# Value projection of eight heads as seven block products, with the raw values parked in DRAM

## The chip, the cores and the metric

One core of one Trainium2 chip runs the whole kernel. The metric is the device time of one launch in microseconds; the clock of TensorE and the busy time of each engine are read from one profiled execution.

## What is computed

Two decoder layers over 512 positions of width 2048. In each layer one projection of x gives queries, keys, values and gates of 12 self-attention heads (six with a forget bias, six sparse with a top-128 selection by an indexer), indexer queries and keys, and queries and gates of four heads into a memory of 256 tokens. The change touches the values alone:

```python
(fq, fk, fv, fg, f_logit, dq, dk, dv, dg, iq, ik, iw, mq, mg) = jnp.split(h, offsets, axis=-1)   # h = x @ w_in
...
y_fox = fox_attention(heads(fq, H_FOX), heads(fk, H_FOX), heads(fv, H_FOX), cum_logf)
...
y = jnp.concatenate([y_fox, y_dsa, y_mem], axis=-1)
y = jnp.einsum('bsn,nd->bsd', y, w_out)
return layer_norm(ALPHA * x + y, ln_gain, ln_bias)
```

All values are float32. Products run as three float32r products of split operands (high times high, high times low, low times high).

## The kernel before, in words

**Chunks.** All weights lie in DRAM as a row of chunks of 128 x 2048 numbers (1 MB). Of each layer the order is: `mv` x4 and `mk` x4 (values and keys of the memory), four pairs `mq`, `mg`, then `small`, `iq` x8 (indexer), and per self-attention head a gate, a query and a key chunk; ahead of heads 0, 4 and 8 stand four `val` chunks that give the values of four heads (512 columns). The output projection (`out`) ends the layer. It already runs as seven products of blocks for each pair of column blocks (Strassen-Winograd, table `PRODUCTS`), with its sums of weight blocks T1 to T4 made beforehand by DMAs from DRAM to DRAM that add on the way (`weight_sums`, on GpSimd's queue). `pool_waits` paces them: a tiny copy on VectorE, then a tiny product on GpSimd, then the DMA.

**The stream.** The main loop goes over the chunks; half a chunk (`h` 0 or 1) has number n. At its start `load_w(i + 2)` issues the load of a later chunk on SyncE's queue, `split_w(n + 3)` splits a later half (ScalarE writes the high part `whi`, VectorE the low part `wlo`), then come the matmuls. There are three raw buffers and four for split halves, so TensorE's splits run at most three halves ahead. Each engine, SyncE's queue too, takes its instructions in the order in which the program issues them.

**Ticks.** Side work (attention, indexer, sums, operands, `next_x`) is a set of generators; `tick()` lets each make a step after either half of a chunk. With `half` it passes over those begun with `whole=True`.

**Slots.** All other tiles of 128 x 512 come from one pool of 69 slots. An instruction whose output finds no free slot waits, on its engine, until one is given back.

**Values.** A `val` chunk has 48 matmuls with 512 columns (two halves, four blocks of rows, two blocks of the sum, three products each). Behind the fourth one the four banks are split at once into `vh`, `vl`, which the heads read.

**Layer change.** `next_x` normalises the residual, transposes it back (16 blocks k, two per tick, during `mv` and `mk` of layer 1), and makes `xf` and its split `xh`, `xl`: 32 slots that hold x of the layer.

Of the kernel before, what the change touches and what calls it, by code (L numbers as in the profile page):

```python
# [11 lines left out]
F32 = mybir.dt.float32  # L12
F32R = mybir.dt.float32r
# [4 lines left out]
P = 128  # L18
# [48 lines left out]

OUT_ORDER = (("P1", 0), ("P1", 1), ("P7", 0), ("P7", 1), ("Q6", 0), ("Q6", 1), ("Q4", 0), ("Q4", 1),
             ("Q5", 0), ("Q5", 1), ("P2", 0), ("Q3", 0), ("P2", 1), ("Q3", 1))


def layer_chunks(l):

    out = []
    for j in range(H_MEM):
        out += [("mq", l, j, MQ + j * HD), ("mg", l, j, MG + j * HD)]
    out.append(("small", l, 0, None))
    for j in range(8):
        out.append(("iq", l, j, IQ + j * P))
    for n in range(H_FOX + H_DSA):  # L80
        if n % 4 == 0:
            out += [("val", l, n // 4, g) for g in range(4)]
        if n < H_FOX:
            h, kinds = n, (("fg", FG), ("fq", FQ), ("fk", FK))
        else:
            h, kinds = n - H_FOX, (("dg", DG), ("dq", DQ), ("dk", DK))
        out += [(kind, l, h, base + h * HD) for kind, base in kinds]
    for dc in range(4):
        for g in range(4):
            out.append(("out", l, dc, g))  # L90
    return out
# [12 lines left out]
def stream():  # L104

    wall = all_chunks()
    where = {c: i for i, c in enumerate(wall)}
    out = []
    for i, c in enumerate(wall):
        kind, l = c[:2]  # L110
        if kind != "out":
            out.append((*c, ("wall", i)))
        elif c == ("out", l, 0, 0):
            for name, pair in OUT_ORDER:
                right = PRODUCTS[name][2]
                for g in range(2):
                    if isinstance(right, str):
                        src = ("sum", (l, right, pair, g))
                    else:
                        src = ("wall", where["out", l, 2 * pair + right[1], 2 * right[0] + g])  # L120
                    out.append((kind, l, (name, pair), g, src))
    return out


# [15 lines left out]
def kernel(  # L140
# [156 lines left out]
    def weight_sums(l):  # L297

        every = [(pair, g) for pair in range(2) for g in range(2)]
        for name, first, second in (("T1", (0, 0), (0, 1)), ("T3", (0, 1), (1, 1)),  # L300
                                    ("T2", "T1", (1, 1)), ("T4", "T2", (1, 0))):
            for step in (first, second):
                for pair, g in every:
                    key = (l, name, pair, g)
                    if isinstance(step, str):
                        src = sums[l, step, pair, g]
                    else:
                        src = wall[where["out", l, 2 * pair + step[1], 2 * step[0] + g]]
                    pool_waits()
                    if step is second:  # L310
# [4 lines left out]
                    yield 2  # L315

    crow_d = [dram.tile([H_FOX, SEQ], F32, name=f"crow{l}") for l in range(DEPTH)]
    x1_d = dram.tile([SEQ, DM], F32, name="x1")


    active = []

    def begin(gen, wait=0, last=False, whole=False):


        active.append([wait, gen, last, whole])

    def tick(half=False):
        for a in sorted(active, key=lambda a: a[2]):
            if half and a[3]:  # L330
                continue
            if a[0] > 0:
                a[0] -= 1
# [304 lines left out]
            yield 1  # L638


    z, stats = {}, {}

    def load_res(l, st, dc):
# [25 lines left out]
    def next_x():  # L669

        ms = [norm_stats(st) for st in range(4)]
        for c in range(4):
            for st in range(4):
                normalise(st, c, *ms[st])
            yield 1
        for k in range(KT):
            c, o = divmod(k, 4)
            tp = bank("xt")
            for st in range(4):
                nc.tensor.transpose(tp[:, st * P:(st + 1) * P], z[st, c][:, o * P:(o + 1) * P], ident)  # L680
            xf, hi, lo = slot("xf"), slot("xh", F32R), slot("xl", F32R)
            nc.scalar.activation(xf, tp, AF.Identity, bias=gcol[:, 1, k:k + 1],
                                 scale=gcol[:, 0, k:k + 1])
            nc.scalar.activation(hi, xf, AF.Copy)
            eng = nc.gpsimd if k % 2 else nc.vector
            eng.tensor_tensor(lo, xf, hi.bitcast(F32), op=ALU.subtract)
            xT[k] = (hi, lo)
            if k % 2:
                yield 1
        yield 6  # L690
        load_rows(0)
        yield 2
# [75 lines left out]
    def weight_cols(n, kk):  # L768
        return tuple(a[:, kk * P:(kk + 1) * P] for a in parts[n])

    for i, (kind, l, j, col, _) in enumerate(chunks):
        late = last_half(i)
        if kind == "out":
            step = OUT_ORDER.index(j)
            name, pair = j
            chain, aname, _, targets = PRODUCTS[name]
            opens = name in ("P1", "P2", "Q6")
            if col == 0:
                if opens:
                    chains[chain, pair] = [bank("z"), bank("z")]  # L780
                zs = chains[chain, pair]

                for st, dc in RES_LOADS.get(step, ()):
                    load_res(l, st, dc)
                if step == 2:
                    begin(late_operands())
        elif kind in ("val", "mv"):
            if col == 0:
                out_ps = {st: bank("v") for st in range(4 if kind == "val" else 2)}
        else:  # L790
            ps = bank("c")
        for h in range(2):
# [35 lines left out]
            elif kind == "out":  # L828
                for st in range(2):
                    for e in range(2):  # L830
                        r = slice(e * 256 + st * P, e * 256 + (st + 1) * P)
                        product(zs[st], tuple(a[:, r] for a in left[aname, 2 * col + h]),
                                tuple(a[:, e * 512:(e + 1) * 512] for a in parts[n]),
                                opens and col == h == e == 0,
                                col == h == e == 1, not opens)
            elif kind == "val":
                for st in range(4):
                    for nn in range(2):
# [24 lines left out]
                            k == 0, k == KT - 1)  # L863
            del parts[n]
            if h == 0:
                tick(kind == "out")
        if kind == "mk":
            t = slot("kmem", F32R)
            split(ps[:, :256], t[:, 0:256], t[:, 256:512])
# [16 lines left out]
        elif kind in ("mg", "fg", "dg"):  # L886
            gate((kind[0], j), ps)
        elif kind == "val" and col == 3:
            vs[j] = []
            for st in range(4):  # L890
                hi, lo = slot("vh", F32R), slot("vl", F32R)
                split(out_ps[st], hi, lo)
                vs[j].append((hi, lo))
        elif kind == "small":
            sm = slot("sm")
            nc.scalar.activation(sm, ps, AF.Copy)
# [128 lines left out]
```

## Time and profile before

| | us |
|---|---|
| median of 3 runs (1987.11 to 1987.69) | 1987.65 |
| the profiled execution, its own time | 1987.82 |
| its span, first to last instruction | 1986.0 |
| TensorE busy in the span | 1970.3 |
| VectorE, ScalarE, GpSimd busy | 1267.4, 732.2, 234.7 |

The profiled execution's own time is 1.8 us over its span (launch and end) and 0.2 us over the median. Busy time of TensorE counts matmuls whose ends are modelled; how densely they stand is read from their starts.

### The profile page before, as it was taken

The numbers are of one execution on the slowest core, as the hardware profiler recorded it, in microseconds if no ns is written. First come the engines' busy times: TensorE is split into PE (matmuls) and PEld (weight loads), VectorE is DVE, ScalarE is ACT, GpSimd is POOL, SyncE is SP. The second block draws the span as 40 slices with busy tenths as digits, with TensorE's granted clock in tenths as the row PEclk, the third lists the DMA queues.
The fourth block names the chain that finished last, engine by engine and source line by source line (L and its number), as shares of the span: only waits on it lengthen the run. The fifth ranks groups of instructions, "written<-read, shape, count | busy, mean of one in ns | idle before, by whom it ended". The sixth has DMA issues, their size and how long they took to land.

```text
span 1986.0 us, 24234 instructions
## 1 busy us (share of the span) xinstructions
PE 1970.3 (99%) x9506; PEld 1677.0 (84%) x9506; DVE 1267.4 (64%) x2069; ACT 732.2 (37%) x1156; POOL 234.7 (12%) x383
## 2 busy tenths in 40 slices
PE   9999999999999999999999999999999999999997
PEld 8889988888888888888898899888888888888886
DVE  6446755678446355688875567456784553567888
ACT  6333344323222222454472333342323232224453
POOL 0000101120110000100038201011201100001101
PEclk9999999999999999999999999999999999999999
DMA  9322355555745322466445324555657362224765
GB/s 371 117 85 78 114 191 133 203 160 191 189 169 151 109 85 85 149 219 241 176 161 200 106 87 156 161 159 181 170 175 199 145 174 102 85 85 164 274 216 151
DMA packets 49966, 316.18 MB, mean 159 GB/s; under 512 B 6576, under 2 KB 6576, under 8 KB 19388
## 3 DMA queue, kind: packets, MB, share of 16 engines
q1 hardware_dynamic: 37596, 226.53, 31.2%
q0 software_dynamic: 12256, 88.11, 17.3%
q8 instruction: 74, 1.21, 0.2%
q14 instruction: 40, 0.33, 0.1%
HBM read 306.20 MB, written 77.62 MB: 193 GB/s over the span
## 4 chain that ended last, share of the span: by engine, by line
PE 97%; DVE 1%; issue 1%; DMA 0%; SPq 0%; ACT 0%; POOL 0%; POOLq 0%; DVEq 0%
PE c L187 20%; PE c L189 19%; PE c L188 19%; PE v L189 5%; PE v L187 5%; PE v L188 5%; PE z L188 5%; PE z L189 5%; PE z L187 5%; PE pt L576 1%; PE po L189 1%; PE po L188 1%; PE po L187 1%; PE ix L503 1%; PE ix L502 1%; PE s L188 1%
## 5 line engine op out<-in xcount | busy, mean ns | idle before, releaser
L187 PE MATMUL c<-xh,whi 128*128 128x512 f32 (+1 forms) x1696 | 650.0, 383 | 0.0
L189 PE MATMUL c<-xh,wlo 128*128 128x512 f32 (+1 forms) x1696 | 647.0, 381 | 0.0
L188 PE MATMUL c<-xl,whi 128*128 128x512 f32 (+1 forms) x1696 | 646.4, 381 | 0.0
L181 DVE TENSOR_TENSOR wlo<-raw,whi 128x1024 fp32r<-128x1024 f32 (+1 forms) x401 | 498.6, 1249 | 199.6 <-ACT whi L180 198.3
L180 ACT ACTIVATE whi<-raw 128x1024 fp32r<-128x1024 f32 (+1 forms) x401 | 419.6, 1052 | 305.1 <-PE v L189 81.8
L189 PEld LDWEIGHTS c<-xh,wlo 128*128 128x128 f32 x1696 | 318.4, 188 | 57.4 <-DVE wlo L181 0.3
L188 PEld LDWEIGHTS c<-xl,whi 128*128 128x128 f32 x1696 | 318.6, 188 | 54.7
L187 PEld LDWEIGHTS c<-xh,whi 128*128 128x128 f32 x1696 | 318.6, 188 | 54.4
L188 PE MATMUL z<-wlo,yh 128*128 128x512 f32 (+1 forms) x434 | 167.9, 387 | 1.2 <-DVE wlo L181 1.2
L187 PE MATMUL z<-whi,yh 128*128 128x512 f32 (+1 forms) x434 | 167.8, 387 | 0.0
L189 PE MATMUL z<-whi,yl 128*128 128x512 f32 (+1 forms) x434 | 167.6, 386 | 0.0
L187 PE MATMUL v<-whi,xh 128*128 128x512 f32 x384 | 150.2, 391 | 0.0
L189 PE MATMUL v<-whi,xl 128*128 128x512 f32 x384 | 149.7, 390 | 0.0
L188 PE MATMUL v<-wlo,xh 128*128 128x512 f32 x384 | 149.5, 389 | 0.0
L188 PEld LDWEIGHTS z<-wlo,yh 128*128 128x128 f32 x434 | 81.5, 188 | 18.3 <-DVE wlo L181 2.0
L189 PEld LDWEIGHTS z<-whi,yl 128*128 128x128 f32 x434 | 81.5, 188 | 16.4
L187 PEld LDWEIGHTS z<-whi,yh 128*128 128x128 f32 x434 | 81.5, 188 | 16.2
L295 POOL TENSOR_TENSOR seen<-mark,mhalf 128x1 f32<-128x1 f32 x64 | 13.6, 212 | 675.0 <-DVE mark L294 562.9
L189 PEld LDWEIGHTS v<-whi,xl 128*128 128x128 f32 x384 | 72.1, 188 | 15.2
L513 DVE SCALAR_TENSOR_TENSOR acc<-rel,iw,acc 128x256 f32<-128x256 f32 (+2 forms) x90 | 51.9, 615 | 51.6 <-ACT rel L507 51.6
L188 PEld LDWEIGHTS v<-wlo,xh 128*128 128x128 f32 x384 | 72.1, 188 | 14.8
L187 PEld LDWEIGHTS v<-whi,xh 128*128 128x128 f32 x384 | 72.1, 188 | 14.6
(175 smaller groups left out, 2259.2 us busy)
## 6 DMA issues: line engine op xcount, KB each, us to landing
raw<-in_wall_dram SPq DMA_DIRECT2D x167, 1024.0 KB, 5.2
sum<-in_wall_dram POOLq DMA_DIRECT2D x32, 1024.0 KB, 8.6
raw<-sum SPq DMA_DIRECT2D x32, 1024.0 KB, 4.8
memraw<-in_memt_dram SPq DMA_DIRECT2D x16, 256.0 KB, 5.3
xraw<-in_xt_dram SPq DMA_DIRECT2D x16, 256.0 KB, 9.0
z<-in_x_dram POOLq DMA_DIRECT2D x16, 256.0 KB, 5.7
x<-z POOLq DMA_DIRECT2D x16, 256.0 KB, 3.4
z<-x POOLq DMA_DIRECT2D x16, 256.0 KB, 6.4
```

What stands on the lines that cost most here:

```text
L180: nc.scalar.activation(hi, src, AF.Copy)
L181: nc.vector.tensor_tensor(lo, src, hi.bitcast(F32), op=ALU.subtract)
L187: nc.tensor.matmul(ps, ah, bh, start=start, stop=False, skip_group_check=more)
L188: nc.tensor.matmul(ps, ah, bl, start=False, stop=False, skip_group_check=more)
L189: nc.tensor.matmul(ps, al, bh, start=False, stop=stop, skip_group_check=more)
L295: nc.gpsimd.tensor_tensor(seen, mark, mhalf, op=ALU.mult)
L502: nc.tensor.matmul(o, st[:, qb * P:(qb + 1) * P], kh2[:, :w], start=True, stop=False)
L503: nc.tensor.matmul(o, st[:, qb * P:(qb + 1) * P], kl2[:, :w], start=False, stop=True)
L513: nc.vector.scalar_tensor_tensor(a, rel, wq, a, op0=ALU.mult, op1=ALU.add)
L576: nc.tensor.transpose(tp[tb][:, toff + (qb - kt) * P:toff + (qb - kt + 1) * P], pr[b][:, off + kt * P:off + (kt + 1) * P], ident)
```

## The change

The values of heads 0 to 7 (`val` chunks j = 0 and 1) are made right behind the memory heads' chunks, ahead of `small`, as one 512 x 2048 by 2048 x 1024 product in seven block products of two chunks each (kind `vs`, 24 matmuls a chunk, order P1, P2, Q6, P7, Q5, Q4, Q3). Weight sums T1 to T4 for them are made by the same kind of DMA (16 more of 1 MB in each layer), begun at chunk 8 in layer 0 (a step at every tick) and at the first chunk of layer 1 (a step at every second tick). The sums of x blocks (S1 to S4) are made by `val_operands` from x read again from DRAM: from the input in layer 0, in layer 1 from `xt_d`, to which `next_x` now writes each `xf` on SyncE's queue. The results are combined (`val_out`), written raw to DRAM (`v_d`), loaded again one chunk ahead of their heads (`load_v`) and split then (`split_v`). The third group of values is still made by `val` chunks, now ahead of head 6, kept raw, and split at head 8. The indexer's scores begin two `iq` chunks earlier, the sums for `out` begin at `small`, and `mem_head` is passed over at half ticks.

```diff
+VAL_ORDER = ("P1", "P2", "Q6", "P7", "Q5", "Q4", "Q3")
 def layer_chunks(l):
         out += [("mq", l, j, MQ + j * HD), ("mg", l, j, MG + j * HD)]
+    out += [("val", l, j, g) for j in range(2) for g in range(4)]
     out.append(("small", l, 0, None))
     for n in range(H_FOX + H_DSA):
-        if n % 4 == 0:
-            out += [("val", l, n // 4, g) for g in range(4)]
+        if n == H_FOX:
+            out += [("val", l, 2, g) for g in range(4)]
...
+    def load_vx(l, i, *blocks):
+        src = (xt_in if l == 0 else xt_d).rearrange("p (k t c) -> p k t c", k=KT, t=2)
+        for t, kh in blocks:
+            vx[t, kh, i] = slot("vx")
+            nc.sync.dma_start(vx[t, kh, i].rearrange("p (k c) -> p k c", k=2),
+                              src[:, 8 * kh + 2 * i:8 * kh + 2 * i + 2, t, :])
+    def val_operand(name, i, x):
+        vleft[name, i] = slot("vxh", F32R), slot("vxl", F32R)
+        split(x, *vleft[name, i])
+    def val_operands(l):
+        first = ((0, 0), (1, 0), (1, 1))
+        load_vx(l, 0, *first)
+        yield 1
+        for i in range(4):
+            if i < 3:
+                load_vx(l, i + 1, *first)
+            a11, a21, a22 = (vx.pop((*b, i)) for b in first)
+            nc.vector.tensor_tensor(a21, a11, a21, op=ALU.subtract)
+            nc.vector.tensor_tensor(a22, a21, a22, op=ALU.add)
+            vx["S3", i], vx["S2", i] = a21, a22
+            yield 1
+            val_operand("S2", i, a22)
+            yield 1
+        for i in range(4):
+            load_vx(l, i, (0, 0))
+            val_operand("S3", i, vx.pop(("S3", i)))
+            yield 1
...
+    def val_out(name, ps):
+        if name in ("P1", "P7", "Q6"):
+            for st in range(2):
+                vraw[name, st] = slot("vraw")
+                nc.scalar.activation(vraw[name, st], ps[st], AF.Copy)
+        for st in range(2):
+            if name == "P2":
+                vraw[0, st] = slot("vraw")
+                nc.vector.tensor_tensor(vraw[0, st], vraw["P1", st], ps[st], op=ALU.add)
+            elif name in ("Q4", "Q5", "Q3"):
+                first, key = {"Q4": ("Q6", (0, 2 + st)), "Q5": ("P7", (1, 2 + st)),
+                              "Q3": ("P1", (1, st))}[name]
+                t = vraw[key] = vraw.pop((first, st))
+                nc.vector.tensor_tensor(t, ps[st], t, op=ALU.subtract)
+        for key in [k for k in vraw if k[0] in (0, 1)]:
+            nc.sync.dma_start(v_d[key], vraw.pop(key))
+    def load_v(j):
+        for st in range(4):
+            vraw[j, st] = slot("vraw")
+            nc.sync.dma_start(vraw[j, st], v_d[j, st])
...
     def next_x():
             nc.scalar.activation(xf, tp, AF.Identity, bias=gcol[:, 1, k:k + 1],
                                  scale=gcol[:, 0, k:k + 1])
+            nc.sync.dma_start(xt_d[:, k * SEQ:(k + 1) * SEQ], xf)
             nc.scalar.activation(hi, xf, AF.Copy)
...
+            elif kind == "vs":
+                for st in range(2):
+                    for e in range(2):
+                        product(zs[st], val_left(aname, 2 * col + h, e, st),
+                                tuple(a[:, e * 512:(e + 1) * 512] for a in parts[n]),
+                                opens and col == h == e == 0, col == h == e == 1, not opens)
...
-            if j == 7:
+            if j == 5:
                 begin(index_scores(l), 2, last=True)
         if kind == "mg":
-            begin(mem_head(l, j))
+            begin(mem_head(l, j), whole=True)
-        if kind == "val" and j == col == 0:
-            begin(weight_sums(l))
+        if i == (8 if l == 0 else first[l]):
+            begin(weight_sums("val", l, range(1), ("T1", "T2", "T3", "T4"), 1 + l))
+        if kind == "mg" and j == H_MEM - 2:
+            begin(val_operands(l))
+        if kind == "small":
+            chains.clear()
+            begin(weight_sums("out", l, range(2), ("T1", "T3", "T2", "T4"), 2))
+        if kind in ("fk", "dk"):
+            n = j if kind == "fk" else H_FOX + j
+            if n % 4 == 0:
+                begin(split_v(n // 4))
+        if kind == "fq" and j % 4 == 0:
+            load_v(j // 4)
```

## Rows read from the trace of the kernel before

**Rows 1.** Page, part 1: busy time, share, instructions of two engines.
```profile
PE 1970.3 (99%) x9506; PEld 1677.0 (84%) x9506; DVE 1267.4 (64%) x2069; ACT 732.2 (37%) x1156; POOL 234.7 (12%) x383
```
**Rows 2.** Waits of TensorE's matmuls, whole span: us in total, times, longest.
```profile
PE z L188 <- DVE wlo L181: 1.2, 2, 0.6
...
PE c L189 <- DVE wlo L181: 0.3, 1, 0.3
```
**Rows 3.** Timeline of TensorE in a val chunk: start, duration; 37 matmuls.
```profile
479.68 0.39 PE L188 MATMUL v<-wlo,xh 128*128 128x512 f32 x1
...
487.84 0.39 PE L188 MATMUL v<-wlo,xh 128*128 128x512 f32 x1
```
**Rows 4.** Groups of instructions, whole span: count, busy us, mean ns.
```profile
L181 DVE TENSOR_TENSOR wlo<-raw,whi 128x1024 fp32r<-128x1024 f32 (+1 forms) x401 | 498.6, 1249 | 199.6 <-ACT whi L180 198.3
L180 ACT ACTIVATE whi<-raw 128x1024 fp32r<-128x1024 f32 (+1 forms) x401 | 419.6, 1052 | 305.1 <-PE v L189 81.8 <-PE c L188 75.6 <-PE z L189 74.0
...
L187 PE MATMUL v<-whi,xh 128*128 128x512 f32 x384 | 150.2, 391 | 0.0
...
L181 DVE TENSOR_TENSOR yl<-y,yh 128x512 fp32r<-128x512 f32 x56 | 38.0, 685 | 5.6 <-ACT yh L180 5.6
...
L713 DVE TENSOR_TENSOR z<-z,z 128x512 f32<-128x512 f32 (+1 forms) x34 | 22.4, 660 | 1.7 <-PE z L189 1.7
```
**Rows 5.** Windows: out stage of layer 0, and the mq/mg chunks; last: DMA.
```profile
66.00:153.60 87.60, 87.60 (x423) 73.71 (x422) 36.73 (x59) 26.58 (x51) 0.00 (x0) 1.00 0.23 84
...
838.00:990.00 152.00, 152.00 (x681) 126.18 (x680) 126.93 (x179) 77.79 (x98) 2.38 (x5) 1.00 0.60 214
```
**Rows 6.** DMA queues and issues, 455 to 530 us: median us to landing last.
```profile
q0 software_dynamic: 519, 7.14, 36.9%
...
raw<-in_wall_dram SPq DMA_DIRECT2D x7, 1024.0 KB, 5.8
sum<-in_wall_dram POOLq DMA_DIRECT2D x3, 1024.0 KB, 8.6
...
sum<-sum POOLq DMA_DIRECT2D x4, 5.4
```
**Rows 7.** The same, 62 to 165 us.
```profile
q1 hardware_dynamic: 1152, 8.39, 22.5%
...
raw<-in_wall_dram SPq DMA_DIRECT2D x8, 1024.0 KB, 4.8
```
**Rows 8.** The same, 235 to 330 us.
```profile
raw<-in_wall_dram SPq DMA_DIRECT2D x8, 1024.0 KB, 7.0
```
**Rows 9.** SyncE's weight loads, 994 to 1030 us: duration ns, first and last start.
```profile
L203 SPq DMA_DIRECT2D raw<-in_wall_dram x6: 327/328/328, 994.5 to 1026.4; - x6
...
DMA to landing us min/median/max: 4.7/4.8/5.3
```
**Rows 10.** Chain that ended last, at the layer change: start, us, what; 8 transposes.
```profile
997.50 0.88 PE xt L680 x8
...
1023.21 0.87 PE xt L680 x8
```
**Rows 11.** The same chain, finer, in the mk chunks.
```profile
1029.95 0.12 PE c L188
```
**Rows 12.** Timeline of ScalarE at the layer change.
```profile
999.32 0.76 ACT L682 ACTIVATE xf<-xt,gcol 128x512 f32<-128x512 f32 x1
...
1004.27 1.05 ACT L180 ACTIVATE whi<-raw 128x1024 fp32r<-128x1024 f32 x1
...
1006.56 0.76 ACT L682 ACTIVATE xf<-xt,gcol 128x512 f32<-128x512 f32 x1
...
1011.51 1.05 ACT L180 ACTIVATE whi<-raw 128x1024 fp32r<-128x1024 f32 x1
```
**Rows 13.** Timeline of VectorE, same stretch.
```profile
1028.63 1.23 DVE L181 TENSOR_TENSOR wlo<-raw,whi 128x1024 fp32r<-128x1024 f32 x1 [1.71 <-ACT whi L180]
```
**Rows 14.** Timeline of ScalarE, a little later: the bracket is idle time before.
```profile
1033.47 0.38 ACT L180 ACTIVATE kmem<-c 128x256 fp32r<-128x256 f32 x1 [4.87 <-PE c L189]
```

More of the change, by code (lines that the diff above doesn't have):

```diff
@@ L108, in stream, with product @@
     out = []
-    for i, c in enumerate(wall):
-        kind, l = c[:2]
-        if kind != "out":
-            out.append((*c, ("wall", i)))
[L113 to L121, printed above, removed]
+    def product(kind, l, name, pair):
+        right = PRODUCTS[name][2]
+        for g in range(2):
+            if isinstance(right, str):
+                src = ("sum", (kind, l, right, pair, g))
+            else:
+                src = ("wall", where[kind, l, 2 * pair + right[1], 2 * right[0] + g])
+            out.append(({"val": "vs"}.get(kind, kind), l, (name, pair), g, src))
+    for i, c in enumerate(wall):
+        kind, l, j = c[:3]
+        if kind == "out":
+            if c == ("out", l, 0, 0):
+                for name, pair in OUT_ORDER:
+                    product("out", l, name, pair)
+        elif kind == "val" and j < 2:
+            if c == ("val", l, 0, 0):
+                for name in VAL_ORDER:
+                    product("val", l, name, 0)
+        else:
+            out.append((*c, ("wall", i)))
     return out
@@ L295, in pool_waits, with weight_sums @@
         nc.gpsimd.tensor_tensor(seen, mark, mhalf, op=ALU.mult)
[L297 to L302, printed above, removed]
+    def weight_sums(kind, l, pairs, names, pause):
+        every = [(pair, g) for pair in pairs for g in range(2)]
+        steps = {"T1": ((0, 0), (0, 1)), "T3": ((0, 1), (1, 1)), "T2": ("T1", (1, 1)),
+                 "T4": ("T2", (1, 0))}
+        for name in names:
+            for n, step in enumerate(steps[name]):
                 for pair, g in every:
-                    key = (l, name, pair, g)
+                    key = (kind, l, name, pair, g)
                     if isinstance(step, str):
-                        src = sums[l, step, pair, g]
+                        src = sums[kind, l, step, pair, g]
                     else:
-                        src = wall[where["out", l, 2 * pair + step[1], 2 * step[0] + g]]
+                        src = wall[where[kind, l, 2 * pair + step[1], 2 * step[0] + g]]
                     pool_waits()
-                    if step is second:
+                    if n:
                         nc.gpsimd.dma_start(sums[key], src, accum_op=ALU.add, max_dma_last_dim=4 * DM)
@@ L314, in weight_sums @@
                         nc.gpsimd.dma_start(sums[key], src)
-                    yield 2
+                    yield pause
     crow_d = [dram.tile([H_FOX, SEQ], F32, name=f"crow{l}") for l in range(DEPTH)]
     x1_d = dram.tile([SEQ, DM], F32, name="x1")
+    v_d = {(j, st): dram.tile([P, 512], F32, name=f"v{j}{st}") for j in range(2) for st in range(4)}
+    xt_d = dram.tile([P, KT * SEQ], F32, name="xt1")
     active = []
@@ L638, in late_operands @@
             yield 1
+    vx, vleft, vraw = {}, {}, {}
+    def load_vx(l, i, *blocks):
[7 more added lines that the diff above has]
+        split(x, *vleft[name, i])
@@ new lines, in val_operands @@
+    def val_operands(l):
[16 more added lines that the diff above has]
+            yield 1
+        for i in range(4):
+            load_vx(l, i, (0, 1))
+            t = vx.pop((0, 0, i))
+            nc.vector.tensor_tensor(t, t, vx["S2", i], op=ALU.subtract)
+            val_operand("S1", i, t)
+            yield 1
+        for i in range(4):
+            t = vx.pop((0, 1, i))
+            nc.vector.tensor_tensor(t, t, vx.pop(("S2", i)), op=ALU.subtract)
+            val_operand("S4", i, t)
+            yield 2
@@ new lines, in val_left @@
+    def val_left(name, i, e, st):
+        if name in ("A11", "A12", "A22"):
+            t, kh = int(name[1]) - 1, int(name[2]) - 1
+            c = t * 256 + st * P
+            return tuple(a[:, c:c + P] for a in xT[8 * kh + 2 * i + e])
+        c = e * 256 + st * P
+        return tuple(a[:, c:c + P] for a in vleft[name, i])
+    def val_out(name, ps):
[14 more added lines that the diff above has]
+            nc.sync.dma_start(v_d[key], vraw.pop(key))
@@ L641, with split_v @@
+    def load_v(j):
+        for st in range(4):
+            vraw[j, st] = slot("vraw")
+            nc.sync.dma_start(vraw[j, st], v_d[j, st])
+    def split_v(j):
+        vs[j] = []
+        for st in range(4):
+            hi, lo = slot("vh", F32R), slot("vl", F32R)
+            split(vraw.pop((j, st)), hi, lo)
+            vs[j].append((hi, lo))
+            yield 1
     z, stats = {}, {}
@@ L769, in weight_cols @@
         return tuple(a[:, kk * P:(kk + 1) * P] for a in parts[n])
+    first = {l: min(i for i, c in enumerate(chunks) if c[1] == l) for l in range(DEPTH)}
     for i, (kind, l, j, col, _) in enumerate(chunks):
@@ L786 @@
                     begin(late_operands())
+        elif kind == "vs":
+            name = j[0]
+            chain, aname = PRODUCTS[name][:2]
+            opens = name in ("P1", "P2", "Q6")
+            if col == 0:
+                if opens:
+                    chains[chain] = [bank("v"), bank("v")]
+                zs = chains[chain]
         elif kind in ("val", "mv"):
@@ L835 @@
                                 col == h == e == 1, not opens)
+            elif kind == "vs":
+                for st in range(2):
[3 more added lines that the diff above has]
+                                opens and col == h == e == 0, col == h == e == 1, not opens)
             elif kind == "val":
@@ L865 @@
             if h == 0:
-                tick(kind == "out")
+                tick(kind in ("out", "vs"))
         if kind == "mk":
@@ L888 @@
         elif kind == "val" and col == 3:
-            vs[j] = []
             for st in range(4):
-                hi, lo = slot("vh", F32R), slot("vl", F32R)
-                split(out_ps[st], hi, lo)
-                vs[j].append((hi, lo))
+                vraw[j, st] = slot("vraw")
+                nc.scalar.activation(vraw[j, st], out_ps[st], AF.Copy)
+        elif kind == "vs" and col == 1:
+            val_out(name, zs)
         elif kind == "small":
```

## The prediction

> **What bounds the kernel now.** I read the busy table first: TensorE is busy 1970.3 of 1986.0 us and VectorE 1267.4 [rows 1]. Busy time alone proves little, since its matmuls overlap, so the waits of TensorE come next: everything it waits for inside the span adds up to a few microseconds, the late low parts of a split weight at 1.2 us and less [rows 2]. Then the starts: 37 matmuls with 512 columns stand between 479.68 and 487.84 us, 36 steps, so 0.2267 us from start to start [rows 3]. The stage is a dense row of matmuls at a granted clock of 1.00 (the last column but two of the windows, [rows 5]); there, time is the number of matmuls, and what matters beside it is only what opens a gap in the row.
>
> **What is removed.** A val group is 64 products of three matmuls (384 products in each row of the group list, for six groups [rows 4]). Two groups are 128 products a layer; seven products of blocks in two chunks of 8 products are 112. That is 16 products, 48 matmuls fewer a layer: 48 x 0.2267 = 10.88 us, and 21.76 us for both. The weight loads into the array go with them. Nothing else on TensorE is added.
>
> **What is added beside it, costed at nothing.** Per layer, VectorE gets 12 more low parts of weights (14 chunks in place of 8) at 1.249 us, 16 differences and 16 low parts of operands at about 0.685 us, and 8 combinations out of PSUM at 0.660 us [rows 4]: 15.0 + 21.9 + 5.3 = 42 us. Most falls into the seven products, 14 chunks x 24 x 0.2267 = 76.2 us. There VectorE does 28 low parts (35.0), 26 of the 32 operand steps (17.8), the combinations (5.3) and about 2 us of the last memory head: 60 of 76.2 us, 79%. The out stage of layer 0 has the same chunk of 24 matmuls with VectorE at 126.9 of 152 us, 83%, and TensorE busy throughout [rows 5]; that is the cover. Were it gone, the products would run at VectorE's pace: nothing until its work passes 76 us, and then what it passes them by. ScalarE's 28 high parts take 29.5 us of the same 76 us and leave more room.
>
> The 16 sums a layer take 36.9% of 75 us for seven, 3.95 us of all DMA engines each [rows 6]. In layer 0 they fall into the mq/mg chunks, where the DMA share is 0.23 of 87.6 us [rows 5]: 20 + 63 = 83 us of 87.6. Loads will land late there, but each chunk lasts 11 us and three raw buffers cover over 20. The earlier indexer, the third group's later split and the reload of raw values are under chunks of 11 to 14 us with the same three-half lead (over 16 us); I cost them at nothing, and if that lead is used up they cost what the rival on slots says.
>
> **The layer change, where I expect the loss.** Here a queue is passed: `next_x` now puts 16 writes of `xf` on SyncE's queue, and each waits for ScalarE. Before, the six weight loads between 994.5 and 1026.4 us were issued as soon as a raw buffer came free and landed in 4.8 us [rows 9]. Now the load of chunk mk0 (and of mk1, mk2, mk3 in the same way) stands behind two writes, so it is issued only when the second `xf` of the tick is there. ScalarE has no room: from the high part of mk0's first half at 1004.27 to that of mk1 at 1011.51 it takes 7.24 us of back-to-back work, about the time of the chunk [rows 12]. Going round once: `whi` starts at 1004.27, the second `xf` of the next tick ends at 1006.56 + 0.76 = 1007.32, 3.05 us later; with the issue of a write and of the load (0.33 us each [rows 9]) the load leaves 3.45 to 3.7 us after the `whi`. It lands L later and the next `whi` of a first half is due 7.24 us after the last. So ScalarE waits L + 3.6 - 7.24, about L - 3.7, four times (mk0: `xf` ends at 1000.08, load at 1000.5, due at 1004.27, the same L - 3.8 within a tenth; I use 3.8). Behind the waiting `whi` stand the next `xf`, so the next load: the waits add.
>
> TensorE has some slack against that: the low part of mk3's first half was ready at 1028.63 + 1.23 = 1029.86 [rows 13], and TensorE came to it after the last transposes, at 1023.21 + 0.87 + three half chunks of 24 matmuls at 0.12 us [rows 10, 11] = 1032.7, so 2.8 us. Loss = 4 x (L - 3.8) - 2.8. The wait of 4.87 us that ScalarE has at 1033.47 for a slot [rows 14] comes after this half is split and gives nothing back.
>
> What is L? Alone a load takes 4.8 us [rows 7, 9]; then the loss is 1.2 us. But the sums of layer 1 start in just these chunks, one per chunk of some 7 us. With a sum about every 11 us loads take 5.8 us [rows 6], in another such stretch 7.0 [rows 8]: losses of 5.2 and 10.0 us. The sums come more densely here and two writes of 256 KB go ahead on the same queue, so I take the nearest row, 7.0, and 10.0 us. As the upper bound I take the 8.6 us of an adding sum [rows 6]: 16.4 us.
>
> On this the Trainium skill has a rule that speaks against the change (DMA: Bandwidth & Descriptors, section "Queues, rings and completion order"): each DMA engine goes round between the queues it has work for, packet by packet, so a load beside a sum gets half. A load's own transfer is 22.5% of 103 us for eight, 2.9 us [rows 7]; at half rate that makes L = 4.8 + 2.9 = 7.7 and a loss of 12.8 us in place of 10.0. The trace's 7.0 lies nearer to it than to 4.8.
>
> **The seven products.** Four combinations a layer are written to DRAM by SyncE right where they are made, so the next load waits for the end of a chunk. The worst is P2: I count about 71 tiles live against 69 slots there (x 32, operands 14, raw blocks 8, raw values 4, memory head 9, y 4), so its adds wait for the last memory head's six matmuls, 1.36 us, then 2 x 0.66 [rows 4]. Load at 3.0 us after the chunk, 7.0 to land, 1.05 + 1.25 to split: 12.3 us, and two chunks plus the head are 12.24 us. At the other three it is 11.0 against 10.88. With a write and an operand load ahead I put 0.6 us a layer, 1.2 us in all; below it nothing (loads of 4.8 us), above it 1.7 us at each of eight places with loads of 8.6 us, 13.6 us.
>
> **Sum.** 1987.8 - 21.8 + 10.0 + 1.2 = 1977.2 us for the profiled execution; the median of the runs is 0.2 us under it: 1977.0 us.
>
> **Rivals.** *The loop at the layer change is harmless* (sums and loads hardly meet, L near 4.8): 1987.6 - 21.8 + 1.2 = 1967.0 us. For it: loads land in 4.7 to 5.3 us in that stretch now [rows 9], and the first two sums are plain copies (5.4 us [rows 6]). Against: the sums are new there.
>
> *Slots hold the loads, slower.* Operand loads and raw values ask for slots on SyncE's queue ahead of weight loads. In the seven products the pool is full at two or three chunks. If a load can leave only when the chunk before has been evicted and its operands made, a chunk takes 7.0 + 2.3 + 2 x 0.69, about 10.7 us in place of 5.44, 5.2 us more. With the 10 us of the layer change the gain is gone after (21.8 - 11.2) / 5.2 = 2 such chunks of 28; with six it is 1977 + 31 = 2008 us. For it: the full pool, and ScalarE already waits 4.87 us for a slot today [rows 14]. Against: it falls on P2 mostly, and operands are given back one chunk later.
>
> *The clock falls in the gaps.* Stalls of 3 to 4 us at mk2 and mk3 are longer than any gap now. The Trainium skill (TensorE: Matmul & The Clock Gate, "HAM oscillation") says that waits for loads between bursts bring the half clock back. No row here has such a gap with matmuls behind it; the windows stay at 1.00 [rows 5]. If mk2 and mk3 (96 matmuls at 0.12 us, 11.5 us) ran wholly at half clock, that would be 11.5 us more, 1988.5 us.
>
> *The change does not shorten the row:* if matmuls of the new chunks stood wider than 0.2267 us, by 21.8 / 672 = 0.032 us or 14%, the fewer products would save nothing: 1987.6 + 11.2 = 1999 us. Against it: the out stage has the same form of operands and chunk.
>
> **How the numbers follow.** The forecast, loads of 5.8 to 8.6 us with little else (1971 to 1984), 0.50. The harmless loop (1966 to 1970) 0.22. Slots 0.18, of which 0.04 still faster, 0.05 no change, 0.09 slower. The clock 0.05, half of it still faster. The wider row 0.05, without gain or slower. A measurement of this kernel can tell about 0.2%, 4 us, from no change; that gives 0.78 faster, 0.10 the same, 0.12 slower. The range that leaves out the slots' bad end and the wider row is 1965.5 to 1986 us.
>
> **What would show it.** 48 matmuls of kind val or vs fewer a layer at 0.2267 us; SyncE's loads of mk1 to mk3 issued after the `xf` writes and ScalarE's `whi` waiting for DMA there; TensorE gaps of 3 to 4 us ahead of mk2 and mk3; mk3 starting some 10 us later against mv0 than now; next to no gap in the 76 us of the products. Wrong would be: gaps spread over the products, or loads that land in 5 us despite the sums.

## The result: 18.4 us slower, and the profile after

The changed kernel takes 2005.95 us in the median of four runs (2002.27 to 2009.27), beside 1987.54 us for the kernel before (1987.11 to 1987.69): a ratio of 1.0093, 95% interval 1.0075 to 1.011. The forecast was 1977.0 us, range 1965.5 to 1986, with 0.12 for slower. The time lies 29 us over the forecast and outside the range.

The profiled execution took 2005.69 us, its span 2003.9. Part 1 of its page, to lay beside [rows 1], and the page's line on HBM:

```profile
PE 1960.8 (98%) x9410; PEld 1662.9 (83%) x9410; DVE 1340.5 (67%) x2205; ACT 780.5 (39%) x1232; POOL 276.0 (14%) x447
...
HBM read 367.02 MB, written 119.56 MB: 243 GB/s over the span
```

The 96 matmuls are gone, as forecast. TensorE is busy 9.5 us less, but idle 43.1 us (2003.9 - 1960.8) where it was idle 15.7 (1986.0 - 1970.3). Where before all its waits came to 3.5 us, there is now a longer list (waits of TensorE: line, tile, what it waited for; us in total, times, longest), to lay beside [rows 2]:

```profile
PE c L198 <- ACT whi L191: 9.1, 3, 6.4
PE v L199 <- DVE wlo L192: 6.7, 13, 0.8
PE xt L779 <- DVE vl L192: 3.3, 1, 3.3
PE pt L590 <- DVE bt L582: 2.3, 2, 1.1
PE v L198 <- ACT whi L191: 2.3, 3, 1.1
PE cqt L479 <- DVE crow L474: 1.9, 2, 0.9
PE c L200 <- DVE wlo L192: 1.8, 3, 0.8
...
PE ix L516 <- ACT rel L521: 0.9, 2, 0.5
```

The windows place them (stretch, its length, then busy us of TensorE, weight loads, VectorE, ScalarE, GpSimd; granted clock; DMA share; GB/s): the mq/mg chunks and the out stage as in [rows 5], and, from the first matmul to the last, the seven products of layer 0, the mk chunks at the layer change, the seven products of layer 1. The last line is of the kernel before: its mk chunks at the layer change.

```profile
66.00:153.60 87.60, 87.60 (x423) 73.70 (x422) 40.79 (x79) 27.07 (x52) 13.23 (x29) 1.00 0.94 289
152.66:237.74 85.08, 81.05 (x352) 64.37 (x350) 54.40 (x71) 39.50 (x56) 1.32 (x2) 1.00 0.64 214
828.47:985.93 157.46, 157.46 (x708) 130.90 (x707) 131.29 (x180) 79.15 (x100) 4.50 (x8) 1.00 0.62 218
...
1011.92:1056.86 44.94, 31.81 (x220) 30.67 (x219) 18.31 (x26) 25.43 (x37) 15.62 (x16) 0.85 0.92 280
1156.35:1243.02 86.67, 82.31 (x353) 65.91 (x352) 56.52 (x73) 40.90 (x57) 4.76 (x6) 0.98 0.64 221
```
```profile
1012.61:1039.01 26.40, 26.11 (x220) 25.91 (x219) 16.13 (x18) 19.84 (x29) 9.65 (x12) 1.00 0.42 136
```

In the first window the DMA share rose from 0.23 to 0.94 with TensorE busy throughout: that cover held. Three things did not hold. The mk chunks (192 matmuls from 1011.92 to 1056.86 us) take 44.94 us; in the kernel before the same 192 take 26.41 us: 18.5 us more. The seven products take 85.08 and 86.67 us; run 1 below shows 79.06 for the same work without its stalls: 6.0 + 7.6 = 13.6 us. And three waits behind the `small` chunk and the attention (`cqt`, `pt`, `ix`), absent before, make 1.9 + 2.3 + 0.9 = 5.1 us. With the gain: 1987.8 - 21.8 + 18.5 + 13.6 + 5.1 = 2003.2 us, 2.5 us under the 2005.7 of this execution. Of these, 0.9 us are two waits for split weights right behind the products of layer 0 (0.5 and 0.4 us), the tail of the same stall; the rest I have not placed.

**The seven products, on SyncE's queue** (timeline of its DMA issues: start, time of the stretch, line, transfer, count):

```profile
178.52 0.94 SPq L724 DMA_DIRECT2D v<-vraw  x2
...
218.15 0.92 SPq L724 DMA_DIRECT2D v<-vraw  x2
219.17 0.91 SPq L214 DMA_DIRECT2D raw<-in_wall_dram  x2
```

and on ScalarE (start, time, line; the bracket is its idle time before and what ended it):

```profile
224.40 2.01 ACT L191 ACTIVATE whi<-raw 128x1024 fp32r<-128x1024 f32 x2 [7.19 <-DMA raw<-in_wall_dram]
...
237.05 2.01 ACT L191 ACTIVATE whi<-raw 128x1024 fp32r<-128x1024 f32 x2 [8.20 <-DMA raw<-in_wall_dram]
```

The stores of the combined values (L724) wait on the queue for VectorE's combination (L722); the weight loads behind them, whose buffers had been free, leave only then, two within 0.91 us. The combination itself comes late. The last matmul of product Q5 ends at 213.93 us, that of Q4 at 224.81, but on VectorE other work stands ahead of the combinations (its timeline):

```profile
216.29 1.23 DVE L192 TENSOR_TENSOR wlo<-raw,whi 128x1024 fp32r<-128x1024 f32 x1 [0.26 <-ACT whi L191]
217.44 1.28 DVE L722 TENSOR_TENSOR vraw<-v,vraw 128x512 f32<-128x512 f32 x2
...
225.50 3.67 DVE L192 TENSOR_TENSOR wlo<-raw,whi 128x1024 fp32r<-128x1024 f32 x3 [5.64 <-ACT whi L191]
229.08 1.28 DVE L722 TENSOR_TENSOR vraw<-v,vraw 128x512 f32<-128x512 f32 x2
```

The second pair stands behind three low parts whose weights were held by the store of Q5's values: the loop feeds itself. So the loads behind P2, Q5 and Q4 leave 4.5, 5.2 and 6.0 us after the product's last matmul in layer 0, and 4.5, 5.2 and 6.5 us in layer 1. The three-half lead of split weights is gone when they land.

What the lead had covered then shows. While operands are being made, `whi` stands behind an operand's high part, which waits for VectorE (ScalarE):

```profile
189.64 0.63 ACT L191 ACTIVATE vxh<-vx 128x512 fp32r<-128x512 f32 x1 [1.89 <-DVE vx L690]
190.18 1.04 ACT L191 ACTIVATE whi<-raw 128x1024 fp32r<-128x1024 f32 x1
```

A split half comes every 3.5 us, while 12 matmuls take 2.72. Without lead TensorE follows: from the first stall on, five halves take 17.8 us in layer 0 (187.80 to 205.61 us) and 17.6 in layer 1 (1191.28 to 1208.89), 8.2 us more than their matmuls, the larger part of the 13.6. And in layer 1 the clock falls for 3.4 us behind gaps of 1.15 and 0.76 us, with matmuls 0.43 us apart in place of 0.23:

```profile
1230.48:1233.90 3.42, 3.41 (x8) 2.73 (x9) 3.29 (x4) 2.00 (x2) 0.00 (x0) 0.50 0.00 0
```

**The layer change.** ScalarE waits 13.0 us for three of the four loads among the x writes, which land in 6.8 to 9.0 us instead of 4.7 to 5.3 [rows 9] (group of SyncE's weight loads, 999 to 1037 us):

```profile
  ACT whi L191: 13.0, 3
...
DMA to landing us min/median/max: 6.8/7.7/9.0
```

The last and longest stall has a second cause (ScalarE's timeline):

```profile
1046.72 0.63 ACT L784 ACTIVATE xh<-xf 128x512 fp32r<-128x512 f32 x1 [5.70 <-DMA xt<-xf]
1047.26 1.04 ACT L191 ACTIVATE whi<-raw 128x1024 fp32r<-128x1024 f32 x1
```

Here `xh` waits for a slot that an `xf` still holds until its write to `xt_d` has landed; the `whi` of mk3 stands behind it, and TensorE waits 6.4 us. And the clock fell, three times. These windows begin near the end of the first gap (3.3 us, up to 1022.5); the granted clock is third from the end:

```profile
1022.27:1025.68 3.41, 3.18 (x15) 3.19 (x16) 1.92 (x5) 3.38 (x5) 1.39 (x2) 0.50 0.99 261
1025.68:1035.92 10.24, 7.21 (x59) 6.80 (x58) 3.90 (x6) 5.55 (x10) 3.10 (x3) 1.00 1.01 257
1035.92:1039.34 3.42, 3.42 (x19) 3.42 (x18) 1.52 (x1) 2.44 (x4) 2.82 (x3) 0.50 1.01 284
1039.34:1046.16 6.82, 2.65 (x22) 2.45 (x21) 0.69 (x1) 1.05 (x2) 0.08 (x1) 1.00 0.95 349
1046.16:1052.99 6.83, 4.17 (x18) 3.88 (x19) 2.46 (x4) 3.70 (x5) 1.97 (x3) 0.50 0.85 300
```

The gaps that TensorE has in this stretch add up to 3.3 (`xt`) + 8.6 (`whi`, two) + 1.2 (`wlo`, two) = 13.1 us. Most of the other 5.4 of the 18.5 us is matmuls that stand 0.21 us apart at the 1.2 GHz level (granted clock 0.50) in place of 0.12 at 2.4 GHz.

### The profile page after: what moved, and what is told of

The parts are those of the page before. It is cut to its first block, busy times and chain, and to the rows that moved or that the text cites. A ratio compares the mean times of both kernels' runs of the same rounds, so it can differ in the third digit from the quotient of the medians.

```text
span 2003.9 us, 24622 instructions
## 1 busy us (share of the span) xinstructions
PE 1960.8 (98%) x9410; PEld 1662.9 (83%) x9410; DVE 1340.5 (67%) x2205; ACT 780.5 (39%) x1232; POOL 276.0 (14%) x447
## 5 line engine op out<-in xcount | busy, mean ns | idle before, releaser
L192 DVE TENSOR_TENSOR wlo<-raw,whi 128x1024 fp32r<-128x1024 f32 (+1 forms) x425 | 523.0, 1236 | 244.7 <-ACT whi L191 243.3
L191 ACT ACTIVATE whi<-raw 128x1024 fp32r<-128x1024 f32 (+1 forms) x425 | 443.4, 1052 | 314.4 <-PE z L200 74.0
L306 POOL TENSOR_TENSOR seen<-mark,mhalf 128x1 f32<-128x1 f32 x96 | 31.1, 323 | 863.8 <-DVE mark L305 759.9
L198 PE MATMUL v<-whi,xh 128*128 128x512 f32 x224 | 87.6, 391 | 0.0
L191 ACT ACTIVATE qh<-rope 128x512 fp32r<-128x512 f32 x24 | 15.2, 633 | 185.1 <-DVE rope L427 185.1
L200 PE MATMUL v<-whi,xl 128*128 128x512 f32 x224 | 87.2, 389 | 0.0
L199 PE MATMUL v<-wlo,xh 128*128 128x512 f32 x224 | 87.2, 389 | 0.0
L191 ACT ACTIVATE qh<-c 128x512 fp32r<-128x512 f32 x32 | 19.2, 598 | 146.8 <-PE c L200 141.9
L191 ACT ACTIVATE pth<-pt 128x512 fp32r<-128x512 f32 (+1 forms) x72 | 35.3, 526 | 100.5 <-PE pt L590 98.6
L424 DVE TENSOR_TENSOR rope<-c,tabs 128x512 f32<-128x512 f32 (+2 forms) x42 | 26.8, 639 | 69.0 <-PE c L200 68.7
```

Source lines behind the costliest of these rows:

```text
L191: nc.scalar.activation(hi, src, AF.Copy)
L192: nc.vector.tensor_tensor(lo, src, hi.bitcast(F32), op=ALU.subtract)
L198: nc.tensor.matmul(ps, ah, bh, start=start, stop=False, skip_group_check=more)
L199: nc.tensor.matmul(ps, ah, bl, start=False, stop=False, skip_group_check=more)
L200: nc.tensor.matmul(ps, al, bh, start=False, stop=stop, skip_group_check=more)
L424: nc.vector.tensor_tensor(t1[:rows, c], ps[:rows, c], cos[:rows, c], op=ALU.mult)
```

## The experiments

The theory after the result: both losses come from what stands in order on a queue, stores that wait for a compute engine ahead of weight loads. Rivals: the traffic of the sums slows the loads; the products alternate between ScalarE and VectorE and run at that pace; the pool of slots is full. All runs but the timed two are one time each; the kernel before took 1987.7 to 1988.0 us on the same chips. "Mem stretch" is the time from the first to the last of the 192 mk matmuls at the layer change.

**1. The stores of combined values on GpSimd's queue.**

```diff
-            nc.sync.dma_start(v_d[key], vraw.pop(key))
+            nc.gpsimd.dma_start(v_d[key], vraw.pop(key))
```

> Only the writes of the combined values move from SyncE's queue to GpSimd's. Theory (queue order: weight loads stand behind stores that wait for a chunk's end): the loads of the seven products leave when a raw buffer is free, the stage falls from 85.1 and 86.7 us to 79 to 81 us in both layers (78.4 is its work on TensorE), the layer change keeps its 18 us, total about 1994 to 1996 us. Rival (operand steps that go from VectorE to ScalarE and back bind the stage at 3.5 us a half): the stage stays above 83 us. Rival (more traffic makes loads late wherever they are issued): ScalarE still waits 7 us for loads there and the total stays above 2001 us.

1990.56 us, 15 less than the change and some 4 less than expected. Both product stages run without a gap to speak of (windows):

```profile
154.16:233.21 79.05, 78.94 (x353) 65.11 (x352) 58.45 (x75) 42.00 (x58) 4.65 (x8) 1.00 0.76 255
1149.55:1228.61 79.06, 78.90 (x353) 65.12 (x352) 58.96 (x75) 41.97 (x58) 9.55 (x12) 1.00 0.75 264
```

VectorE does more work than in the stalled stage (58.45 for 54.40 us) and DMA moves more (0.76 for 0.64), in less time: neither the pace of the two engines nor the traffic holds TensorE by itself. The pace is the same here, `whi` at 184.21, 187.68 and 191.16 us (ScalarE):

```profile
187.14 0.63 ACT L191 ACTIVATE vxh<-vx 128x512 fp32r<-128x512 f32 x1 [1.89 <-DVE vx L690]
187.68 1.04 ACT L191 ACTIVATE whi<-raw 128x1024 fp32r<-128x1024 f32 x1
```

But the lead is whole when it begins, and lasts until the operands are made. Seven loads between 207 and 236 us now leave one at a time and nobody waits for them. The mem stretch stays at 44.25 us.

**2. The x writes on GpSimd's queue instead** (stores of values left on SyncE's).

```diff
-            nc.sync.dma_start(xt_d[:, k * SEQ:(k + 1) * SEQ], xf)
+            nc.gpsimd.dma_start(xt_d[:, k * SEQ:(k + 1) * SEQ], xf)
```

> Only the 16 writes of x at the layer change move from SyncE's queue to GpSimd's. Queue order: the loads of mk0 to mk3 leave some 6 to 10 us earlier; from the start of the out stage to the end of mk the 228.4 us fall to 211 to 214 (209.9 before the change), total about 1990 us. Rival (traffic): loads still hold ScalarE, above 222 us. Rival (slots: xf is held until its write has landed, ScalarE waited 5.7 and 0.6 us for that): some 6 us stay, 216 to 218 us.

2003.35 us, mem stretch 43.04 us: a miss for the theory as it stood. ScalarE no longer waits for loads there; it waits for slots, for longer than expected (its waits, 1011 to 1057 us):

```profile
ACT xf L781 <- DMA xt<-xf: 14.9, 3, 8.5
...
ACT xh L784 <- DMA xt<-xf: 3.5, 1, 3.5
```

The writes stand behind the sums on GpSimd's queue and land in 9.6 us in the median. The same loss comes back by way of the slots, so the queue's order is half of the story: where a write is put decides, too, how long it holds its buffer.

**3. Layer 1's sums begun eight chunks later.**

```diff
-        if i == (8 if l == 0 else first[l]):
-            begin(weight_sums("val", ..., 1 + l))
+        if i == 8 + first[l]:
+            begin(weight_sums("val", ..., 1))
```

> The value sums of layer 1 begin eight chunks later, at the first mq chunk, with a step at every tick; the x writes stay on SyncE's queue. Queue order times landing: loads there land in 5 to 5.7 us, so by 4 x (L - 3.8) - 2.8 the loss is 2 to 5 us, out stage to end of mk 212 to 215 us, and no drop of the granted clock; total 1989 to 1993 us. If queue order alone were enough, whatever the landing time, it would stay above 222 us.

2015.22 us, a miss. The mem stretch falls to 35.71 us, 9.2 less where 13 to 16 were expected, and its granted clock is still 0.90. And the sums, now one at every tick beside the loads of operands, put layer 1's products at 103.5 us, where TensorE waits 8.3 + 5.5 us for weights at a granted clock of 0.92. What it does show: without sums about half of the loss at the layer change is left.

**4. The kernel before, with only the 16 x writes on SyncE's queue** (no sums in that stretch).

> The kernel before, with nothing added but the 16 writes of x to DRAM on SyncE's queue at the layer change (nobody reads them). Queue order: loads land in about 5.3 us, loss 2 to 4 us, total 1990 to 1992 us. If the writes harm only together with the sums by traffic: no loss, within 1 us of the kernel before. Slots: a wait of ScalarE for a write's landing at the 15th or 16th block.

1994.66 us, +7.0, more than expected; mem stretch 32.96, +6.6, granted clock 0.95. The writes cost this much without any sums; in it is a wait of 2.8 us of ScalarE for a slot, beside 5.3 us for loads. Loads landed in 5.3 to 5.9 us here; the prediction's 4 x (L - 3.8) - 2.8 gives 4.0 us for their mean of 5.5, and TensorE's waits were 4.5 us.

**5. Run 1 without any x write: layer 1's x blocks are added from the split halves by GpSimd.**

```diff
-            nc.sync.dma_start(xt_d[:, k * SEQ:(k + 1) * SEQ], xf)
...
+            if l:
+                for e in range(2):
+                    hi, lo = (... for a in xT[8 * kh + 2 * i + e])
+                    nc.gpsimd.tensor_tensor(vx[t, kh, i][:, e * 256:(e + 1) * 256], hi, lo, op=ALU.add)
+                continue
```

> The combined values are written by GpSimd's queue as in the first experiment, and x is no longer written to DRAM at the layer change: in layer 1 the blocks of x are added up from their split halves in the slots by GpSimd. The value sums stay where they are. Theory (the writes of x are the whole loss at the layer change, by the queue and by the slot that xf keeps): from the start of the out stage to the end of mk 210 to 212 us (228.4 with the change, 209.9 before), total 1972 to 1977 us. Rival (the sums' traffic makes weight loads late by itself): the stretch stays above 216 us.

1990.08 us, a miss in the total. The mem stretch is 26.41 us, exactly that of before, although the sums run there: their traffic alone costs nothing. The gain is lost again in layer 1's products, 97.40 us. VectorE's differences wait for GpSimd's additions and run long beside them (timelines of the two engines):

```profile
1148.29 5.83 POOL L665 TENSOR_TENSOR vx<-xh,xl 128x256 f32<-128x256 f32 x8
...
1151.42 3.26 DVE L682 TENSOR_TENSOR vx<-vx,vx 128x512 f32<-128x512 f32 x1 [3.71 <-POOL vx L665]
```

**6. Run 1 with the x writes made later**, in the mq/mg chunks of layer 1: high parts written by SyncE, low parts added to them by accumulating DMAs.

> As the fifth, but x still goes through DRAM: its high halves are written by SyncE's queue and its low halves added by GpSimd's queue, both during the mq and mg chunks of layer 1, from tiles that live on anyway. As many bytes as in the change and one write more per block. Theory: the same 210 to 212 us at the layer change, total 1973 to 1979 us. Rival (bytes are the cost): above 1985 us.

1985.65 us, where the rival on bytes had put it. Mem stretch 26.40 us, but with 32 more DMAs beside the sums mq/mg take 105.66 for 97.1 us, with ScalarE waiting 33.2 us for weight loads there, and the products 84.22 us. Whether the bytes or the order on the queues did it was not tried.

**7. Run 5 with the sums for `out` begun in the seventh `iq` chunk** instead of at `small`.

> As the fifth, but the sums for the out stage begin at the seventh iq chunk in place of small, so that GpSimd has no DMA of a sum ahead of the small set-up that the scan of the forget bias waits for. Expected: the gap of 0.9 us ahead of cqt goes in both layers, 1 to 2 us less than the fifth. If the gap is VectorE's own queue, no change.

1987.09 us, 3.0 under run 5. In layer 0 the wait of `cqt` falls from 0.9 to 0.5 us and that of `pt` from 1.1 to 0.8: part of the small waits comes from the earlier start of these sums. In both layers this makes about 1.1 of the 3.0 us; layer 1's products are 1.0 us shorter, and the rest wasn't followed.

**8. The kernel before with the 16 x writes on GpSimd's queue, where no sums stand.**

> The kernel before with only the 16 writes of x, now on GpSimd's queue, where no sum runs at that time. Weight loads are not held, so the queue's part of the fourth experiment's loss (about 4 of 6.6 us) goes; what stays is what slots cost when writes land in 3 to 4 us: total 1988 to 1991 us.

1987.64 us, no loss (the kernel before: 1987.81). DMA issues of this run, then of run 2, 994 to 1045 us (count, KB each, median us to landing):

```profile
xt<-xf POOLq DMA_DIRECT2D x16, 256.0 KB, 4.3
```
```profile
xt<-xf POOLq DMA_DIRECT2D x16, 256.0 KB, 9.6
```

So the writes are harmless on a queue where no sums are ahead of them and no weight loads behind.

**9 to 11. A version from these answers.** Layer 1's sums of value weights depend on no result of layer 0, so they can be made in layer 0, from the second `dg` chunk on, behind the last sum for `out`. Run 9: values' stores and x writes on GpSimd's queue, and

```diff
-        if i == (8 if l == 0 else first[l]):
-            begin(weight_sums("val", ..., 1 + l))
+        if i == 8:
+            begin(weight_sums("val", 0, ..., 1))
+        if l == 0 and kind == "dg" and j == 1:
+            begin(weight_sums("val", 1, ..., 2))
```

> The changed kernel with the v_d stores and the xt_d writes on GpSimd's queue, and with layer 1's sums of value weights begun in the second 'dg' chunk of layer 0, after the last sum of output weights, one each second tick. Theory (both losses come from what stands on a queue behind something slow: stores in front of weight loads on SP's, x writes behind sums on GpSimd's): products stages 79.06 us in both layers as in the run with the v_d stores moved (1990.56), and between the layers the matmuls of mem weights back from 44.25 to 26.40 us as in the kernel before with x writes on GpSimd's queue, so 1990.6 - 17.9 = 1972.7, range 1970 to 1976. Rival (the traffic of sums costs wherever it runs): the stretch from 608 to 836 us and the output stage of layer 0 (220.9 and 157.5 us) grow by some us, 1976 to 1984. Rival (the x writes are slow of themselves in this kernel): the mem stretch stays above 35 us, 1982 or more.

Run 10 adds the later start of run 7:

> The one before (early sums of layer 1, stores and x writes on GpSimd's queue), with the sums of output weights begun in the seventh 'iq' chunk instead of at 'small'. Theory: the small waits after the small chunk shrink as where this was tried (0.5 to 1 us a layer): 1971 to 1972, 1 to 2 us under the version without it. Rival (no effect, or the later sums reach into the early ones of layer 1 and delay the last): within 0.5 us of it or slower.

Run 11 is run 9 with the x writes back on SyncE's queue:

> The version with early sums, but the xt_d writes left on SP's queue, as the change put them. It prices the queue's order at the layer change alone, with no sums beside it. Theory (order on SP's queue 6 to 10 us, the rest of the 18.5 us from the sums beside it): mem stretch 33 us as in the kernel before with x writes on SP's queue, so 6.6 us over the version with both on GpSimd's queue, about 1979. Rival (the whole loss is the queue's order, sums or no sums): mem stretch 42 to 45 us, about 1990. Rival (the whole loss came from the sums): 26.4 us, about 1973.

Run 9: 1974.42 us in the median of five, ratio to before 0.9931 (0.9918 to 0.9943); products 79.10 and 79.92 us, mem stretch 26.40, and the out stage of layer 0 1.9 us longer than before. That, and 0.9 us in layer 1's products, is what the rival on traffic can claim. Run 10: 1972.82 us (1972.21 to 1973.88), 0.9925 (0.9911 to 0.9938), against 1987.95 before. Five runs of the one and five of the other, on one chip, do overlap (1973.06 to 1975.15), so that run 10 gains over run 9 is likely, not shown. Run 11: 1981.28 us, mem stretch 34.79: the order on SyncE's queue without the sums, the slot wait behind it included (4.4 us of ScalarE), costs 8.4 us, and the sums beside it make the rest of the 18.5. Run 10's products of layer 0 take 79.01 us; its mk chunks and its products of layer 1 (windows):

```profile
1005.89:1032.30 26.41, 26.13 (x220) 25.93 (x219) 16.48 (x18) 19.94 (x29) 13.20 (x18) 1.00 0.73 248
1131.87:1210.92 79.05, 78.94 (x353) 65.11 (x352) 58.41 (x74) 42.00 (x58) 3.25 (x6) 1.00 0.63 228
```

Run 11's mk chunks, for the clock:

```profile
1006.12:1040.91 34.79, 29.48 (x220) 28.58 (x219) 16.23 (x19) 21.93 (x32) 9.92 (x12) 0.90 0.66 240
```

Together the runs fill a table of the mem stretch, in us:

| | x writes on SyncE's queue | on GpSimd's queue | no x writes there |
|---|---|---|---|
| sums in the same stretch | 44.94 (the change), 44.25 (run 1) | 43.04 (run 2) | 26.41 (run 5), 26.40 (run 6) |
| no sums there | 32.96 (run 4), 34.79 (run 11) | 26.40 (runs 8, 9) | 26.41 (before) |

## Why the prediction was wrong

**The gain was counted right.** Of 9506 matmuls 9410 are left, and in the new chunks 12 of them take 2.72 us (208.33 to 211.05 us), 0.2267 each. Run 10, without the stalls, is 15.1 us under the kernel before, of the 21.8 us counted: 3.2 us are small waits that it still has, 1.4 us its out stage of layer 0 (158.85 for 157.46 us), and about 2 I have not placed. VectorE's added work stayed covered in run 1, where it is busy 58.5 of 79 us, by the prediction 60 of 76.2. ScalarE, put at 29.5 us, is busy 42.0: the operands' high parts and the copies out of PSUM were not counted, nor that the two engines wait for each other there.

**The step that failed most: the seven products, 1.2 us forecast, 13.6 measured.** The mechanism was named ("written to DRAM by SyncE right where they are made, so the next load waits for the end of a chunk"), and run 1 shows it. Two sizes in it were wrong. The load was to leave 3.0 us after the chunk at P2 and 1.7 us at the other products; in the trace it left 4.5 to 6.5 us after, because the combinations stand on VectorE behind operand steps and behind splits that wait for the load before. The landing was not the error: 5.1 to 6.6 us for the first load behind each store that splits wait for, where I took 7.0. And a stall was priced once, by its own length. But it uses up the lead that covered split halves 3.5 us apart, so the five halves behind it cost 4 us more in each layer. The sentence that the products would run at VectorE's pace only when "its work passes 76 us" looked at VectorE's total, and not at the order in which the two engines hand the operands to each other. That the upper bound in the text is 13.6 us too is luck: it came from loads of 8.6 us at eight places.

**The layer change, 10.0 us forecast, 18.5 measured.** The loop of writes, loads and ScalarE is there: loads issued behind the second `xf`, ScalarE waiting for DMA, gaps ahead of mk2 and mk3. Without sums it costs 6.6 to 8.4 us (runs 4 and 11); with the four loads at 7.8 us in the mean the formula gives 13.2, and the gaps are 13.1. On L, the Trainium skill (DMA: Bandwidth & Descriptors, section "Queues, rings and completion order") was closer than my row: the estimate by its sharing of the DMA engines between queues was 7.7 us, and the median of the four is 7.7, though no run shows the sharing itself. But the agreement of the gaps with the formula is partly luck: the last, 6.4 us, belongs to a slot. The load of mk3 landed at about 1043.2 us and ScalarE, held by `xh`, came to it at 1047.26; some 4 of the 13.1 us are the slot's. I had looked at one slot wait of before and found that it "gives nothing back"; that the 16 writes hold their `xf` slots until they have landed I left out. Run 2 shows that wait alone: 18.4 us of ScalarE, and a loss of 16.6 us.

**The clock, a rival with 0.05, is a term of the sum.** The granted clock fell to 0.50 three times at the layer change, the first time behind a gap of 3.3 us, and most of the 5.4 us outside the gaps are lost by it, of the 11.5 that the rival gave. It fell once more in layer 1's products. The rule named there (the Trainium skill, TensorE: Matmul & The Clock Gate, "HAM oscillation") agrees with the windows: 0.90 in run 11 with a gap of 3.7 us, 0.95 in run 4 with one of 2.2, and 1.00 in run 5's stretch without one. My own forecast had stalls of 3 to 4 us, so its condition was met by the likeliest case, and it belonged there.

**The slots, 0.18,** did not hold the products, which run 1 clears with the same slots. A wait for slots came at the layer change, by another way than named: ScalarE waits for a slot that a write still holds.

**What was costed at nothing.** The dense mq/mg stage held. The earlier indexer and the sums at `small` did not: `cqt`, `pt` and `ix` wait 5.1 us in the change, 3.2 us in run 10 (1.6 of `pt`, 0.8 of `cqt`, 0.8 of `ix`). Starting the sums later gives some of it back; what the rest waits for wasn't tried.

Sum of the misses against the forecast: 12.4 in the products, 8.5 at the layer change, 5.1 in small waits and the 2.5 outside these make the 28.5 us between 1977.2 and 2005.7.

## What to carry to other kernels

A store that waits for a compute engine stops every load issued behind it on the same queue, and what stands ahead of its data on that engine counts too; with two such places, and sums beside one of them, 32 us were lost here, and 32 small DMAs on a queue without weight loads, with the sums out of their way, gave it back. Such a store holds its buffer until it lands, so the queue it goes to must have nothing slow ahead (here the sums): work that depends on no result, like sums of weights, belongs in a stretch with room. A lead that hides a slow stretch is not free to be used up by a stall ahead of it: price the stall and what the lead had covered. And where a forecast has gaps of 2 to 6 us in a dense row of matmuls, the clock's fall goes into the sum, not among the rivals.

## What the runs showed of the hardware

- At the layer change the granted clock went from 1.00 to 0.50 three times, for 3.4, 3.4 and 6.8 us, in or just behind gaps of 3.3, 2.3 and 6.4 us, and was at 1.00 in between. Matmuls of 256 columns then started 0.21 us apart, at 1.00 0.12.
- The length of a gap alone did not tell whether the clock falls: gaps of 1.15 and 0.76 us in layer 1's products were followed by 3.4 us at 0.50, gaps of 1.40 and 0.76 us in run 3's products of layer 0 (223.8 to 226.5 us) were not.
- A DMA share of 0.94 over 87.6 us, 0.23 before, cost TensorE nothing; 16 writes of 256 KB in the wrong order cost 7.0 us (run 4).
- The same write of 256 KB landed in 4.3 us in the median on GpSimd's queue without sums (run 8) and in 9.6 behind sums on it (run 2).
- Beside GpSimd's additions VectorE's difference of 512 columns took 3.26 us; the same kind of operation without them took 0.68 us (run 5).
